# A decoder block on one core: one plain down slab split by two engines, and leftover differences and pair pieces put at other places

## The chip, the cores and the metric

The kernel runs on one core of a Trainium2 chip. A core has a matrix engine (TensorE, PE in the profile, with its weight loads as PEld), a vector engine (VectorE, DVE), a scalar engine (ScalarE, ACT), a general engine (GpSimd, POOL) and a sequencer that issues transfers (SyncE, SP). Each engine works through its own list of instructions in order and waits on semaphores for the others; DMA queues move data between memory and the on-chip buffers. The metric is the time of one execution on the device in microseconds; less is better.

## The reference

One layer of a decoder block over 512 tokens of width 1024, in float32. Two feed-forward halves (SwiGLU, hidden width 2816) enclose a convolution branch and a dilated attention branch; a gated embedding and a last norm follow. The two feed-forward halves are what the change touches:

```python
def swiglu(x, w_gate, w_up, w_down):
    return (jax.nn.silu(x @ w_gate) * (x @ w_up)) @ w_down
...
h = h + 0.5 * swiglu(rms_norm(h, g_ffn1[i]), w_ffn1_gate[i], w_ffn1_up[i], w_ffn1_down[i])
u = rms_norm(h, g_mix[i])
...
h = h + 0.5 * swiglu(rms_norm(h, g_ffn2[i]), w_ffn2_gate[i], w_ffn2_up[i], w_ffn2_down[i])
```

## The kernel before

**Numbers in two halves.** TensorE multiplies rounded numbers, so every operand is split into a rounded high half and the remainder, its low half, and each product is three matmuls: high by high, high by low, low by high. A weight slab of 128 x 1024 is therefore loaded raw (`wr`), and turned into `wh` and `wl`. There are two ways. In `split_one` ScalarE copies the slab into `wh` (rounding it) and VectorE subtracts: `wl = wr - wh` (lines 398 and 399 for products, 419 and 420 for other slabs). In `early_one`, for the slabs that `by_dma` names, ScalarE writes the rounded negative into `wl` (line 368), a DMA issued by POOL adds the raw slab to it on the way (line 370), and ScalarE makes `wh` (line 382). All of `wr`, `wh`, `wl` and some sums take one of 16 buffers of one pool (`NW`), which are handed on in the order in which they come free.

**Seven products for eight.** The gate, up and down products of the feed-forward halves are done in quarters with seven products, called B11, B21, T2, T1, T3, B22 and T4 (`PRODUCTS`). Each needs sums and differences of weight quarters (`sum_one`, VectorE, lines 336 to 349) and of the operands. T1 and T2 read the first differences of the operand, T3 and T4 the second ones. Products share banks of the accumulator: B11, T2, T3 and T4 use `pa`, B21 `pe`, T1 and B22 `pd`, so a product starts when VectorE or ScalarE has taken the one before out of its bank.

**The stages of one feed-forward half** (`ffn`). First come two plain pairs (`plain`, `EARLY` is 2): the first 256 hidden columns, gate and up, without the seven products, over eight chunks of 128 of the input, 6 matmuls each. At given chunks a hook runs: in the first half's second pair, `token` (the norm's statistics of each token, a chain of small VectorE operations that ends with eight diagonals, line 617) at chunk 0, `factor` (two matmuls, lines 622 and 623, that spread the factor over the partitions, and ScalarE's copy of it, `R`) at chunk 4, and `gate` (the products with the factor, silu and the products of gate and up, lines 831 to 834) at chunk 5. Meanwhile `forms` makes the first differences of the operand; its operations lie in the list `jobs`, from which `work` issues as many as fit the matmuls of a chunk by a count of what ScalarE and VectorE have already been given.

Then `PLAN` is followed: units of gate and up (`gu` 2 to 10), rounds of down (`dn` 1 to 5) and, around the last unit, the plain down of the pair that was made without the seven products (`dp` 0 0 and `dp` 0 1, one slab each, `down_plain`):

```python
PLAN = (("gu", 2), ("gu", 3), ("dn", 1), ... ("gu", 8), ("gu", 9),
        ("dn", 4), ("dp", 0, 0), ("gu", 10), ("dp", 0, 1), ("dn", 5))
```

`form_pair` prepares what a unit made for the down products: it lists its pieces in `later`: for B11, for B21 and B22, and for T1 and T2 and for T3 and T4 a ScalarE copy (line 688) and a VectorE split end (line 691) each, and four differences (line 676). The units issue them by `QUOTA` after each product; `down_plain` issues some with its second slab, and `down` forces those that a product still lacks.

**Loads and order.** `slab(key)` hands out the next slab and prepares those behind it in the order of `slab_order`: up to seven ahead are loaded by SP's queue, remainders go out by `LEAD` (5 slabs ahead for T4 and for `dp`, 3 for B11 and B21), and other slabs are split 2 ahead. The program's order is the order on each engine.

Of the kernel before, what the change touches and what calls it, by code (L numbers as in the profile page):

```python
# [22 lines left out]
KD = D // P  # L23
# [41 lines left out]
PRODUCTS = ("B11", "B21", "T2", "T1", "T3", "B22", "T4")  # L65
# [15 lines left out]
POOL_SUMS = False  # L81

POOLED = ("win", "v", "ao", "co")
RAISED = ("dp", "v0")
BY_DMA = ("B11", "B21", "T4")

N_GLU = (0, 0) + (6,) * 14
# [62 lines left out]
def block_kernel(ctx: ExitStack, tc: tile.TileContext, a, out):  # L150
# [44 lines left out]
    order = slab_order()  # L195
# [54 lines left out]
        return max(c.stop for _, c, _ in srcs)  # L250

    def by_dma(key):
        return (product(key) in BY_DMA or key[0] in POOLED + RAISED or key[:2] == ("gq", "2"))

    def product(key):
        return key[2] if key[0] in ("1", "2", "m") else None

    def W(n, dt=F32):
        return wts.tile([P, SLAB], dt, name=name(n), tag="w", bufs=NW)
# [10 lines left out]
    def row_of(srcs):  # L270
        at, out = 0, []
        for src in srcs:
            out.append((None, slice(at, at + src.shape[-1]), src))
            at += src.shape[-1]
        return out
# [85 lines left out]
    def spend(a_=0.0, v=0.0):  # L361
        spent[0] += a_
        spent[1] += v

    def remainder(l, h, srcs):

        spend(0.25 + l.shape[-1] * 0.00075)
        A.activation(l.bitcast(F32R), h, AF.Copy, scale=-1.0)  # L368
        for to, src in places(l, srcs):
            G.dma_start(to, src, accum_op=OP.add)  # L370

    def early_one():
        i = state["early"]
        state["early"] = i + 1
        if by_dma(order[i]):
            r = raws.pop(i)
            l = W("wl", F32R)[:, :r.shape[-1]]
            if product(order[i]) or order[i][0] in RAISED:
                h = W("wh", F32R)[:, :r.shape[-1]]
                remainder(l, r, row_of([r]))  # L380
                spend(0.25 + r.shape[-1] * 0.00075)
                A.activation(h, r, AF.Copy)  # L382
            else:
                h = r
                remainder(l, h.bitcast(F32), sources(order[i]))
            halves[i] = h, l
# [188 lines left out]
    class Norm:  # L575
# [5 lines left out]
        def add(self, t):  # L581
            sq = T("sq")
            A.activation(sq, t, AF.Square)
            self.flush()
            self.last = sq
# [61 lines left out]
    jobs, later = [], []  # L647
# [5 lines left out]
    def next_job(queue=None):  # L653
        f, a_, v = (queue or jobs or later).pop(0)
        if queue is not later:
            spend(a_, v)
        f()
# [9 lines left out]
    def form_pair(x1, x2, parts_, tile_=None, first_of=None, by=V):  # L667


        second, t = [], {"tile": tile_} if first_of is None else first_of  # L670

        def sub(o, half, p_, q_):
            def f():
                if o not in t:
                    t[o] = T("t")
                by.tensor_sub(t[o][:, half], p_(), q_())
            job(f, queue=later)

        def put(names, src):
            w, at = 256 * len(names), []  # L680

            def first_():
                if w == 256:
                    z = T("b", F32R)
                    at.extend((z[:, :256], z[:, 256:]))
                else:
                    at.extend((T("bh", F32R), T("bl", F32R)))
                A.activation(at[0], src(), AF.Copy)

            def end():  # L690
                V.tensor_sub(at[1], src(), at[0].bitcast(F32))
                for i, q in enumerate(names):
                    parts_[q] = tuple(z[:, i * 256:(i + 1) * 256] for z in at)
            job(first_, queue=later)
            second.append(lambda: job(end, queue=later))

        def next_():
            second.pop(0)()

        def t1():  # L700
            sub(0, lo, lambda: x1[:, hi], lambda: x1[:, lo])

        def t2():
            sub(0, hi, lambda: x2[:, hi], lambda: t[0][:, lo])

        def t34():
            sub(1, lo, lambda: x2[:, hi], lambda: x1[:, hi])
            sub(1, hi, lambda: x2[:, lo], lambda: t[0][:, hi])

        if x2 is None:  # L710
            put(("B11",), lambda: x1[:, lo])
            t1()
            next_()
            put(("T1",), lambda: t[0][:, lo])
            next_()
            return t
        if first_of is None:
            put(("B11",), lambda: x1[:, lo])
            put(("B21", "B22"), lambda: x2)
            t1()  # L720
            t2()
            next_()
            put(("T1", "T2"), lambda: t[0])
            next_()
            t34()
        else:
            t2()
            put(("B21", "B22"), lambda: x2)
            put(("T2",), lambda: t[0][:, hi])
            next_()  # L730
            t34()
            next_()
        if first_of is None:
            next_()
        put(("T3", "T4"), lambda: t[1])
        next_()
        job(t.clear, queue=later)
# [50 lines left out]
    def ffn(n, xs, u, norm, out_, soon_=None, last_=None):  # L788
# [95 lines left out]
        def token():  # L884
            y = norm.by_token()
            t = tiny("half", NB)
            V.tensor_scalar(t, y, 0.5, None, op0=OP.mult)
            half_r.append(t)
# [4 lines left out]
        def first():  # L893
            others.append(forms())

        def gate():
            rest = jobs[:]
            jobs.clear()
            gated(*done.pop(0))
            while jobs:  # L900
                next_job()
            jobs.extend(rest)

        done, others = [], []
        hooks = {(0, 1): {k: turns.pop(0) for k in range(KD)}, (1, 0): {0: token, 4: factor, 5: gate}} if n == "1" else {
            (0, 0): {2: soon_, 3: first}, (0, 1): {1: token, 6: factor}, (1, 0): {0: gate}}
        for j in range(EARLY):
            ps = []
# [66 lines left out]
        def down(r):  # L975

            at, k_ = ROUNDS[r]
            ps = banks()
            last = r == len(ROUNDS) - 1
            for q in PRODUCTS:  # L980
                wh, wl = slab((n, ("dn", r), q))
                for k in range(k_):
                    while q not in pairs.get(at + k, ()):
                        next_job(later)
                p = ps[BANKS[q]]
                rows_of(p, q, wh, wl, [pairs[at + k].pop(q) for k in range(k_)], last_[0] if last and q == "T4" else None)
                add(q, p, half_r[0])
                if last and q == "T4":
                    last_[1]()
                for f in ending:  # L990
                    f()
                ending[:] = [lambda q=q: finish(out_, q)] if last and q in FINAL else []
                work(k_ * 1.3)

        def down_plain(r, x_):
            at, k_ = (2 * z for z in ROUNDS[r])
            wh, wl = (z.rearrange("p (m k i) -> p k m i", m=4, k=k_) for z in slab(("dp", n, r, x_)))
            for two in ((0, 1), (2, 3)):
                while any(at + i not in hid for i in range(k_)):
                    next_job(later)  # L1000
                each = [(bank("pd"), b, slice(b * P, (b + 1) * P)) for b in two]
                for p, b, c in each:
                    for i in range(k_):
                        PE.matmul(p, hid[at + i][0][:, c], wh[:, i], start=i == 0, stop=False)
                        PE.matmul(p, hid[at + i][1][:, c], wh[:, i], start=False, stop=False)
                for p, b, c in each:
                    for i in range(k_):
                        PE.matmul(p, hid[at + i][0][:, c], wl[:, i], start=False, stop=i == k_ - 1)
                for _ in range(min(6 * x_, len(later))):
                    next_job(later)  # L1010
                for p, b, c in each:
                    t = h[b][:, x_ * S:(x_ + 1) * S]
                    V.scalar_tensor_tensor(t, p, half_r[0][:, b:b + 1], t, op0=OP.mult, op1=OP.add)
                spend(0, 1.5)
                work(2 * k_ * 0.68)
            if x_:
                hid.clear()
# [103 lines left out]
    turns = [lambda b=b, j=j: row_block(b, j) for j in (1, 0) for b in reversed(range(NB))]  # L1121
# [66 lines left out]
    for c in range(KD):  # L1188
        z = c, bank("pb"), bank("pa"), T("gg"), T("glu")
        if c == 0:  # L1190
            ws = [take(("win", m)) for m in (8, 0)]
            for k in range(KD):
# [4 lines left out]
                i = slice(k * P, (k + 1) * P)  # L1197
# [245 lines left out]
    for s in range(NSLOT):  # L1443
        q, k = [], []
# [4 lines left out]
        v0 = T("v0")  # L1449
# [13 lines left out]
        n = 1  # L1463
# [12 lines left out]
        v0 = None  # L1476
        q = k = None
# [79 lines left out]
    n = 0  # L1557
# [163 lines left out]
    for k in range(KD):  # L1721
        j, two = k % 2, (k // 2 * 2, k // 2 * 2 + 1)
# [84 lines left out]
```

## Time and profile before

| | us |
|---|---|
| Median of 3 runs | 1277.58 |
| Lowest and highest of them | 1277.21, 1277.71 |
| The profiled execution | 1279.57 |
| Its span, first to last instruction | 1277.8 |
| Granted TensorE clock, mean share | 0.996 |
| VectorE busy | 1051.6 |
| ScalarE busy | 743.3 |
| Software DMA queue (POOL's), share of 16 engines | 54.3% |

In the rows of a timeline the first number is the start in us from the start of the span, the second the time that the row's instructions take together, then come engine, line, operation, what is written from what, and a count; in brackets stands how long the engine was idle before and what ended that. In rows of waits the numbers after the colon are us in total, times and the longest. In a row of stretches the pairs are busy us and instructions of PE, PEld, DVE, ACT and POOL, then the granted TensorE clock, the DMA share and GB/s.

### The profile page before, as it was taken

How to read it: one execution, taken by the hardware profiler on the slowest of the kernel's cores; microseconds unless marked ns; L12 is line 12 of the kernel's file. 1: busy time of each engine (PE TensorE's matmuls, PEld its weight loads, DVE VectorE, ACT ScalarE, POOL GpSimd, SP SyncE). 2: the span in 40 equal slices, each digit the busy share in tenths (PEclk: the TensorE clock that was granted, in tenths of full speed). 3: DMA queues.
4: the chain of work that ended last, by engine and by line, in shares of the span. 5: the costliest groups of instructions: out<-in, count | busy, mean ns of one | idle time of the engine just before them, and what ended most of it. 6: DMA issues, size and time to landing. Idle time of an engine off the chain costs nothing.

```text
span 1277.8 us, 19737 instructions
## 1 busy us (share of the span) xinstructions
PE 1261.8 (99%) x7394; PEld 1118.8 (88%) x7394; DVE 1051.6 (82%) x1713; ACT 743.3 (58%) x1084; POOL 237.7 (19%) x310
## 2 busy tenths in 40 slices
PE   9999999999999999999999999999999999999997
PEld 7898999998888889889898888878898999998886
DVE  6898988897889988888888654797688988897975
ACT  6576666575643354747565545465576666665563
POOL 0011111111222232323332222124111111111000
PEclk9999999999999999999999999999999999999999
DMA  7378778688788899888888777759677778677531
GB/s 270 83 169 211 167 184 202 157 195 217 171 188 203 187 181 193 158 187 153 173 176 190 170 165 184 196 128 278 140 163 199 173 186 207 156 201 184 149 99 66
DMA packets 121702, 225.45 MB, mean 176 GB/s; under 512 B 19208, under 2 KB 63624, under 8 KB 121608
## 3 DMA queue, kind: packets, MB, share of 16 engines
q0 software_dynamic: 48160, 141.58, 54.3%
q1 hardware_dynamic: 73160, 82.37, 20.2%
q8 instruction: 58, 0.95, 0.3%
q14 instruction: 36, 0.29, 0.1%
q10 hardware_dynamic: 288, 0.26, 0.1%
HBM read 168.56 MB, written 2.13 MB: 134 GB/s over the span
## 4 chain that ended last, share of the span: by engine, by line
PE 88%; DVE 5%; DMA 2%; issue 2%; ACT 2%; DVEq 0%; POOLq 0%; ACTq 0%
PE pa L748 5%; PE pa L745 5%; PE pa L746 5%; PE pq L470 4%; PE pq L471 4%; PE pq L472 4%; PE pg L471 3%; PE pg L470 3%; PE pg L472 3%; PE pa L755 3%; PE pa L756 3%; PE pa L760 3%; PE pd L746 2%; PE pd L748 2%; PE pd L745 2%
## 5 line engine op out<-in xcount | busy, mean ns | idle before, releaser
L370 POOL DMA_DIRECT2D wl<-wr x98 | 84.6, 863 | 606.1 <-ACT wl L368 433.2
L1154 DVE SCALAR_TENSOR_TENSOR acc<-glu,taps,acc 128x511 f32<-128x511 f32 (+14 forms) x240 | 161.3, 733 | 0.0
L399 DVE TENSOR_TENSOR wl<-s,wh 128x1024 fp32r<-128x1024 f32 x90 | 109.9, 1221 | 41.6 <-ACT wh L398 32.2
L368 ACT ACTIVATE wl<-wh 128x1024 fp32r<-128x1024 f32 x84 | 87.9, 1051 | 72.8 <-DMA wh<-in_w_in 41.3
L368 ACT ACTIVATE wl<-wr 128x1024 fp32r<-128x1024 f32 x98 | 102.9, 1050 | 17.6 <-DVE wl L399 6.8
L745 PE MATMUL pa<-bh,wh 128*128 128x256 f32 x432 | 106.8, 285 | 3.2 <-DVE p L956 3.2
L382 ACT ACTIVATE wh<-wr 128x1024 fp32r<-128x1024 f32 x98 | 102.6, 1047 | 10.4 <-PE pd L760 7.4
L746 PE MATMUL pa<-bl,wh 128*128 128x256 f32 x432 | 106.7, 284 | 0.0
L398 ACT ACTIVATE wh<-s 128x1024 fp32r<-128x1024 f32 x90 | 94.0, 1049 | 21.2 <-PE pd L756 9.5
L370 POOL DMA_DIRECT2D wl<-in_w_in x56 | 48.7, 870 | 225.4 <-ACT wl L368 219.9
L470 PE MATMUL pq<-xsh,wh 128*128 128x512 f32 x224 | 88.7, 396 | 0.0
L471 PE MATMUL pq<-xsl,wh 128*128 128x512 f32 x224 | 87.3, 390 | 0.0
L472 PE MATMUL pq<-xsh,wl 128*128 128x512 f32 x224 | 87.3, 390 | 0.0
L745 PEld LDWEIGHTS pa<-bh,wh 128*128 128x128 f32 x432 | 83.3, 193 | 3.6 <-DVE p L956 3.6
L746 PEld LDWEIGHTS pa<-bl,wh 128*128 128x128 f32 x432 | 83.5, 193 | 0.0
L470 PE MATMUL pg<-xsh,wh 128*128 128x512 f32 x192 | 76.9, 401 | 0.3 <-DVE tg L831 0.2
L471 PE MATMUL pg<-xsl,wh 128*128 128x512 f32 x192 | 75.3, 392 | 0.7 <-DVE xsl L499 0.6
L472 PE MATMUL pg<-xsh,wl 128*128 128x512 f32 x192 | 75.0, 391 | 0.0
L943 ACT ACTIVATE p<-pa 128x512 f32<-128x512 f32 x36 | 21.5, 596 | 74.4 <-PE pa L748 74.0
L748 PE MATMUL pa<-bh,wl 128*128 128x256 f32 x432 | 61.4, 286 | 0.0
L771 DVE SCALAR_TENSOR_TENSOR gx<-pa,half,gx 128x512 f32<-128x512 f32 x80 | 56.3, 747 | 1.6 <-PE pa L760 1.3
L748 PEld LDWEIGHTS pa<-bh,wl 128*128 128x128 f32 x432 | 56.5, 195 | 0.0
(363 smaller groups left out, 3829.7 us busy)
## 6 DMA issues: line engine op xcount, KB each, us to landing
wl<-wr POOLq DMA_DIRECT2D x98, 512.0 KB, 5.2
wh<-in_w_in POOLq DMA_DIRECT2D x56, 512.0 KB, 7.3
wl<-in_w_in POOLq DMA_DIRECT2D x56, 512.0 KB, 6.5
wr<-in_w_ffn_down SPq DMA_DIRECT2D x44, 512.0 KB, 5.3
wr<-in_w_ffn_up SPq DMA_DIRECT2D x80, 256.0 KB, 4.5
wr<-in_w_ffn_gate SPq DMA_DIRECT2D x78, 256.0 KB, 4.9
wh<-in_w_v POOLq DMA_DIRECT2D x16, 256.0 KB, 7.1
wl<-in_w_v POOLq DMA_DIRECT2D x16, 256.0 KB, 5.1
```

The source lines that it names most:

```text
L368: A.activation(l.bitcast(F32R), h, AF.Copy, scale=-1.0)
L370: G.dma_start(to, src, accum_op=OP.add)
L382: A.activation(h, r, AF.Copy)
L398: A.activation(h, r, AF.Copy)
L399: V.tensor_sub(l, r, h.bitcast(F32))
L470: PE.matmul(ps, wh, xh, start=start, stop=False, skip_group_check=part)
L471: PE.matmul(ps, wh, xl, start=False, stop=False, skip_group_check=part)
L472: PE.matmul(ps, wl, xh, start=False, stop=stop, skip_group_check=part)
L745: PE.matmul(o, h[:, c], th, start=q in ("B11", "B21", "T1") and i == 0, stop=False, skip_group_check=True)
L746: PE.matmul(o, h[:, c], tl, start=False, stop=False, skip_group_check=True)
L748: PE.matmul(o, l[:, c], th, start=False, stop=i >= len(at) - 2, skip_group_check=True)
L1154: bg.append(lambda acc=acc, g=g, w=w, s=s: V.scalar_tensor_tensor(acc[:, s:], g[:, :S - s], w, acc[:, s:], op0=OP.mult, op1=OP.add))
```

## The change

Three things are changed.

The first slab of the plain down (`dp` 0 0, in both halves) leaves the names that are split with a DMA; `split_one` does it with ScalarE and VectorE, two slabs ahead. The second slab (`dp` 0 1) stays with the DMA.

In the second plain pair of the first half, the hook of chunk 0 first issues what is left of the first differences up to the last ScalarE copy, then `token`; `factor` and `gate` stand one chunk later.

In `form_pair` the split end of T1 and T2 stands ahead of the two second differences. With the second slab of the plain down, 2 pieces instead of 6 are issued after its second half, and up to 3 each after B11 and B21 of the last round of down.

```diff
-RAISED = ("dp", "v0")
+RAISED = ("v0",)
...
     def by_dma(key):
-        return (product(key) in BY_DMA or key[0] in POOLED + RAISED or key[:2] == ("gq", "2"))
+        return (product(key) in BY_DMA or key[0] in POOLED + RAISED or key[:2] == ("gq", "2")
+                or key[0] == "dp" and key[3])
...
-            if product(order[i]) or order[i][0] in RAISED:
+            if product(order[i]) or order[i][0] in RAISED + ("dp",):
...
             put(("T1", "T2"), lambda: t[0])
             next_()
+            next_()
             t34()
         else:
...
             t34()
-            next_()
-        if first_of is None:
             next_()
         put(("T3", "T4"), lambda: t[1])
...
+        def soon_first():
+            while any(a_ for _, a_, _ in jobs):
+                next_job()
+            token()
...
-        hooks = {(0, 1): {k: turns.pop(0) for k in range(KD)}, (1, 0): {0: token, 4: factor, 5: gate}} if n == "1" else {
+        hooks = {(0, 1): {k: turns.pop(0) for k in range(KD)}, (1, 0): {0: soon_first, 5: factor, 6: gate}} if n == "1" else {
...
                 add(q, p, half_r[0])
+                if last and q in PRODUCTS[:2]:
+                    for _ in range(min(3, len(later))):
+                        next_job(later)
...
-                for _ in range(min(6 * x_, len(later))):
+                for _ in range(min((6 if two[0] == 0 else 2) * x_, len(later))):
                     next_job(later)
```

## The prediction

> **What bounds the kernel now.** I read the page first, then the waits of TensorE over the whole span, then the timelines of the stretches in which those waits lie.
>
> ```profile
> span 1277.8 us, 19737 instructions
> PE 1261.8 (99%) x7394; PEld 1118.8 (88%) x7394; DVE 1051.6 (82%) x1713; ACT 743.3 (58%) x1084; POOL 237.7 (19%) x310
> ...
> PE pa L745 <- DVE p L956: 3.2, 2, 1.8
> ...
> PE pd L748 <- DVE wl L399: 1.0, 1, 1.0
> PE pa L755 <- DVE gx L771: 0.8, 1, 0.8
> ...
> PE R L623 <- DVE diag L617: 0.2, 1, 0.2
> ```
>
> TensorE is busy 99% of the span, and the kernel leaves its matmuls as they are. So the change can only win or lose at the few places where TensorE stands still (16 us in all, ramp and tail included), and an instruction that goes elsewhere is worth nothing. The rows name four such places near the edits: the second plain pair of the first FFN (L623), the last unit of each FFN (L956 twice, L399 once) and the last round of the first FFN (L771). I take the edits by these places.
>
> **The first differences and the token norm, first FFN.**
>
> ```profile
> 35.88 0.16 DVE L645 SCALAR_TENSOR_TENSOR m<-rows 128x4 f32<-128x4 f32 x1 [0.79 <-ACT sq L641]
> ...
> 39.34 0.88 DVE L617 TENSOR_SCALAR diag<-ident,yl 128x128 fp32r<-128x128 f32 x4
> ...
> 40.20 0.70 DVE L846 TENSOR_TENSOR bl<-t,bh 128x512 fp32r<-128x512 f32 x1
> ...
> 41.60 0.68 DVE L846 TENSOR_TENSOR bl<-t,bh 128x512 fp32r<-128x512 f32 x1
> ...
> 45.68 0.69 DVE L831 TENSOR_TENSOR tg<-pg,R 128x512 f32<-128x512 f32 x1
> ```
> ```profile
> 39.13 0.39 PE L472 MATMUL pu<-xsh,wl 128*128 128x512 f32 x1
> 39.58 0.47 PE L622 MATMUL R<-diag,one_r 128*128 128x512 f32 x1
> 40.28 0.50 PE L623 MATMUL R<-diag,one_r 128*128 128x512 f32 x1 [0.23 <-DVE diag L617]
> 40.62 0.39 PE L470 MATMUL pg<-xsh,wh 128*128 128x512 f32 x1
> ...
> 45.85 0.39 PE L472 MATMUL pu<-xsh,wl 128*128 128x512 f32 x1
> ...
> 46.42 0.50 PE L470 MATMUL pg<-xsh,wh 128*128 128x512 f32 x1 [0.18 <-DVE tg L831]
> ```
>
> From 40.62 to 45.85 are 23 matmuls, 0.227 us each. Three steps after 39.13 is 39.81, but the plain matmuls go on at 40.62: **0.81 us** are lost because factor's two matmuls (L622, L623) stand at chunk 4 and the diagonals are ready only at 40.2. At the next pair TensorE starts at 46.42 instead of 46.08, since its bank comes free with the first L831; the loss lies between the 0.18 of the row and 0.34, and I take **0.24**.
>
> The change puts one split end and two differences (40.20 to 41.60, 1.40 us) and one ScalarE copy (a later row) ahead of the token norm. VectorE stood idle 0.79 us before L645, so the norm starts 0.6 later at most and its last diagonal ends near 40.8. Factor now stands one chunk later, six matmuls or 1.36 us: at 40.72 for L622 and 40.95 for L623. Both find their diagonal; the margin is 0.1 to 0.2 us. Gate, too, moves one chunk back, to about 42.1, but what it waits for comes earlier:
>
> ```profile
> 41.72 0.63 ACT L843 ACTIVATE bh<-t 128x512 fp32r<-128x512 f32 x1 [5.87 <-DVE t L856]
> ```
>
> ScalarE sat 5.87 us behind this copy, with the split of the next slab and the copy of R queued after it. Issued before the norm it runs near 36.5, and VectorE's list after the norm is one split end, one slab subtraction and two split ends (0.6 + 1.14 + 1.2 from 40.8), so that L831 runs near 43.7 instead of 45.68. TensorE wants its bank at 45.3. No DMA is moved by this; SP's and POOL's queues keep their order. Both losses go: **-1.05 us**; the bounds are nothing and -1.15. Behind it no wait of TensorE is named until the last unit at 316 us, and its loads are released by TensorE itself, so the gain should travel.
>
> **The order of the pair's pieces and the quotas, last round of each FFN.**
>
> ```profile
> 328.09 0.68 DVE L691 TENSOR_TENSOR bl<-u,bh 128x512 fp32r<-128x512 f32 x1
> 328.69 0.42 DVE L676 TENSOR_TENSOR t<-u 128x256 f32<-128x256 f32 x1
> ...
> 330.75 1.40 DVE L1013 SCALAR_TENSOR_TENSOR gx<-pd,half,gx 128x512 f32<-128x512 f32 x2
> 332.07 1.22 DVE L399 TENSOR_TENSOR wl<-s,wh 128x1024 fp32r<-128x1024 f32 x1
> 333.21 1.40 DVE L771 SCALAR_TENSOR_TENSOR gx<-pa,half,gx 128x512 f32<-128x512 f32 x2
> ...
> 338.11 1.41 DVE L771 SCALAR_TENSOR_TENSOR gx<-pa,half,gx 128x512 f32<-128x512 f32 x2
> ```
> ```profile
> 332.22 1.07 PE L760 MATMUL pe<-wl,bh 128*128 128x512 f32 x4
> 334.10 0.47 PE L755 MATMUL pa<-wh,bh 128*128 128x512 f32 x1 [0.81 <-DVE gx L771]
> ...
> 337.09 0.39 PE L755 MATMUL pd<-wh,bh 128*128 128x512 f32 x1
> ```
>
> T2 could start at 332.22 + 4 x 0.227 = 333.13 and end 12 x 0.227 later, at 335.85; the next product starts at 337.09, so **1.24 us** are lost, to an add of B11 that VectorE begins at 333.21. Ahead of it VectorE does, between the two halves of the plain down, six pieces from 328.09 to 330.75 (2.66 us). With the new order and the quota of 2 it does two split ends there (0.60 each, as from 328.09 to 328.69), so the second half's add begins near 329.3, the slab subtraction near 330.6 and B11's add near 331.75. T2 then finds its bank. The other pieces (two differences of 0.33, one split end of 0.60) follow the adds of B11 and B21, still ahead of T3, the first to need them. VectorE has no slack here, so part comes back: counting on, T2's add ends near 339.3 as before, while T3 now wants the bank at 338.6 and its second half at 339.05: 0.4 us of new wait. Net **-0.85 us**, bounds 0 and -1.24. In the second FFN no L771 wait is shown, because TensorE already comes late there: 0. In the other units the same pieces only swap places within one quota: 0, hidden by VectorE's idle time.
>
> **The plain down's first slab.** Removed per FFN: one ScalarE copy, one POOL issue and its 512 KB DMA. Added: one VectorE subtraction, and the remaining copy moves two slabs later.
>
> ```profile
> 286.11 1.07 ACT L368 ACTIVATE wl<-wr 128x1024 fp32r<-128x1024 f32 x1 [0.75 <-PE pd L756]
> ```
> ```profile
> L420 DVE TENSOR_TENSOR wl<-wr,wh x9: 1215/1226/2023, 16.5 to 1215.6; 128x1024 fp32r<-128x1024 f32 x9
> ```
> ```profile
> 300.16 1.41 DVE L1013 SCALAR_TENSOR_TENSOR gx<-pd,half,gx 128x512 f32<-128x512 f32 x2 [1.31 <-PE pd L1008]
> ...
> 1160.92 1.41 DVE L1013 SCALAR_TENSOR_TENSOR gx<-pd,half,gx 128x512 f32<-128x512 f32 x2 [1.14 <-PE pd L1008]
> ```
>
> The subtraction takes 1.22 us, 1.14 in a row of others, right behind T3's add in the fourth round. Queued behind it are the sums for the last unit and the adds of B22, T4 and the first half; all are late by up to 1.1 us, and the idle 1.31 and 1.14 us before the second half's add swallow that. The matmuls that read the low half come some 5 us after it. So 0, with bounds of -0.3 and +1.1 in each FFN, were that cover gone. ScalarE's 1.05 us and POOL's issue free nobody: the next remainders there go out earlier, but no TensorE wait hangs on them.
>
> **What stays: the last unit.**
>
> ```profile
> 307.10 0.85 POOL L370 DMA_DIRECT2D wl<-wr  x1 [11.64 <-ACT wl L368]
> ```
> ```profile
> 314.96 1.23 DVE L399 TENSOR_TENSOR wl<-s,wh 128x1024 fp32r<-128x1024 f32 x1 [3.88 <-DMA wl<-wr]
> ...
> 1177.32 1.23 DVE L399 TENSOR_TENSOR wl<-s,wh 128x1024 fp32r<-128x1024 f32 x1 [5.48 <-DMA wl<-wr]
> ```
> ```profile
> 310.26 1.05 ACT L398 ACTIVATE wh<-s 128x1024 fp32r<-128x1024 f32 x1
> ...
> 313.10 0.59 ACT L943 ACTIVATE p<-pd 128x512 f32<-128x512 f32 x1
> ```
> ```profile
> 310.00:320.00 10.00, 8.60 (x72) 8.40 (x71) 6.12 (x10) 6.22 (x8) 1.70 (x2) 1.00 1.02 263
> ```
> ```profile
> 1181.00:1184.60 3.60, 3.00 (x18) 3.00 (x19) 3.56 (x6) 0.77 (x1) 0.86 (x1) 0.73 0.64 123
> 1184.60:1188.00 3.40, 3.40 (x17) 3.06 (x17) 3.40 (x5) 3.36 (x5) 0.86 (x1) 0.78 0.39 119
> ```
>
> The dear waits are here. B22's low half is written into a weight buffer that T4's remainder DMA still reads; VectorE stands 3.88 and 5.48 us for its landing, and TensorE then waits for the add behind it (1.4 and 1.8, and 1.0 before that in the second FFN). That DMA goes out at 307.10 beside the round's loads, long after the removed one (its copy at 286.11) has landed, and all of these are released by TensorE. I see nothing in the change that moves them relative to each other: 0. After the second of these waits the granted clock (the column ahead of the DMA share) is 0.73 over 3.6 us and 0.78 over 3.4 us, which costs 0.97 + 0.75 = 1.7 us more.
>
> **The sum** against the profiled execution (1279.57 us, of it span 1277.8): -1.05 - 0.85 = -1.9 us. It ran 2.0 us above the median of the runs, so I take the difference alone to the median: 1277.6 - 1.9 = **1275.7 us**, 0.15% less. A measurement of this kernel can tell about 0.2%, 2.6 us, from no change.
>
> **Rivals.**
>
> *Only one gain holds* (0.12). L623 has a margin of 0.1 to 0.2 us, and VectorE is full in the last round. Either gain alone gives 1276.5 to 1276.7.
>
> *The clock drop goes* (0.13). The second FFN's stands still come 1.9 us earlier, and if TensorE's clock then isn't lowered, 1.7 us go as well: 1274.0. For it: in the first FFN a wait of 1.4 us lowered nothing (granted clock 1.00 from 310 to 320). Against: the waits themselves stay. The Trainium skill (TensorE: Matmul & The Clock Gate, part 1) says that the clock is halved after an idle window of some 3.4 us, and that the windows run freely; by that no single wait here is long enough, yet the rows show the drop, worth 3.4 us at half rate, so its phase, not only the wait's length, seems to decide.
>
> *The landing in the last unit comes sooner* (0.12), with less DMA traffic ahead. If the second FFN's came like the first's (1.6 us sooner: 5.48 against 3.88 of idle), the 1.0 us wait and the clock's 1.7 go: 1273.0; without any such wait, a further 1.4 + 1.8 less: 1269.8. Against: the removed DMA ended long before.
>
> *Slower: B22's copy takes that buffer* (0.08). The removed tiles change the order in which the 16 weight buffers come round. If the one that T4's DMA reads falls to B22's high half (L398, now at 310.26) instead of the low one, ScalarE stands till 314.9, and behind it are a remainder's two copies and the L943 of 313.10, which has to empty pd before B22. L943 then ends near 318.5, B22 runs 2.9 us and T4 starts near 321.4, not 319.2: +2 us in each FFN, and the clock's 1.7 in the first: +5.7 - 1.9, 1281.4. It decides from the point where that buffer is freed one place earlier in the order. Against: I count the buffers to come round in the same order, two of them exchanged.
>
> *The edits change nothing that TensorE waits for* (0.05): 1277.6.
>
> **Chances.** The forecast holds 0.50, with a range of its own of 1274.9 to 1276.5; about 0.05 of it lies beyond 0.2%. Faster by over 0.2%: 0.05 + 0.13 + 0.12 = 0.30. Slower: 0.08, and 0.02 for the subtraction uncovered in both FFNs without the gains. Within: 0.60. The range leaves out the slow rival and the far end of the sooner landing: 1271.8 to 1278.2.
>
> **What would show it.** Right: in the changed profile no wait of L623 on L617, no 0.81 at L755 of T2 in the last round, L831 near 43.7, and L399's waits for DMA wl<-wr unchanged. Wrong: a wait of TensorE on the new subtraction, L398 waiting for a wl DMA in the last unit, or a PEclk of 1.0 after the second last unit.

## The result and the profile after

The changed kernel takes **1286.28 us** (median of 6 runs, 1283.34 to 1288.91) against 1277.64 us of the kernel before on the same chip (6 runs, 1277.21 to 1279.27): a ratio of 1.0066, with an interval from 1.0051 to 1.0081. It was forecast 0.15% faster; it is 0.66% slower. Line numbers from 253 to 725 have grown by one (L399 is now L400, L688 now L689), those from 734 to 893 are as before (L755, L760 and L771 among them), and the later ones have grown by five to eight.

First the page and the waits of TensorE of the changed kernel:

```profile
span 1281.6 us, 19727 instructions
PE 1261.4 (98%) x7394; PEld 1117.6 (87%) x7394; DVE 1053.8 (82%) x1715; ACT 742.6 (58%) x1082; POOL 236.8 (18%) x308
...
PE pe L760 <- DMA wl<-wr: 3.8, 3, 1.4
PE pa L755 <- ACT wh L399: 3.6, 2, 1.8
PE pa L745 <- DVE p L961: 1.9, 2, 1.4
```

TensorE's work is the same. The waits named for the start (L623, L831) and for T2's bank (L771) are gone, as forecast. Two new ones stand first: three waits for a remainder DMA at B21 (`pe`), and two at T3, one in each FFN.

Both traces hold 7394 matmuls. Taken in the order of their starts, the n-th of the one can be set beside the n-th of the other; the difference of the two starts shows where time is lost. The last column is the same for the last kernel of the experiments below.

| start in before, us | what has passed | after minus before, us | last kernel minus before, us |
|---|---|---|---|
| 47.00 | token norm of the first FFN | -1.14 | -1.12 |
| 102.10 | up to B21 of round one | -0.74 | -0.81 |
| 104.14 | B21 of round one | +0.66 | -0.81 |
| 280.01 | up to B21 of round four | +0.67 | -0.81 |
| 283.19 | B21 of round four | +2.39 | -0.81 |
| 330.18 | the last unit | +1.50 | +0.13 |
| 339.58 | T2 of the last round | +0.26 | -1.11 |
| 342.07 | T3 of the last round | +2.48 | -0.63 |
| 1140.09 | second FFN, up to round four's B21 | +3.06 | +0.37 |
| 1142.13 | B21 of round four | +4.61 | +0.37 |
| 1189.05 | the last unit | +1.55 | -3.10 |
| 1202.19 | T2 of the last round | +1.55 | -3.09 |
| 1210.00 | T3 of the last round | +3.78 | -2.61 |

So B21 costs 1.40 + 1.72 + 1.55 = 4.67 us in three rounds, and T3 2.22 + 2.23 = 4.45 us. Against this stand the start (1.14), T2 (1.24) and the last units. Two smaller losses lie between the rows. Of the 1.14 us, 0.40 are gone before round one; the kernel with the hook alone loses 0.33 there too, and neither trace names a cause. Behind T3 of the first FFN another 0.70 are lost at 350.89, where a plain product waits 0.43 us for a DMA (L473 on `wl<-in_w_in`): ScalarE prepares the first two remainders of that stage at 341.84 and 345.18, in the kernel before at 338.68 and 340.12. No other kernel here has this wait.

The table compares the two profiled executions, which are 3.8 us apart. The medians are 8.6 us apart: the profiled execution of the kernel before lies 1.9 us above its median, that of the changed kernel 2.9 us below.

**Why B21 waits.** ScalarE's timeline before round four, first of the kernel before, then of the changed one:

```profile
270.87 0.63 ACT L688 ACTIVATE bh<-t 128x512 fp32r<-128x512 f32 x1 [0.91 <-DVE t L676]
271.40 1.05 ACT L368 ACTIVATE wl<-wr 128x1024 fp32r<-128x1024 f32 x1
```
```profile
273.87 0.63 ACT L689 ACTIVATE bh<-t 128x512 fp32r<-128x512 f32 x1 [3.25 <-DVE t L677]
274.41 1.04 ACT L369 ACTIVATE wl<-wr 128x1024 fp32r<-128x1024 f32 x1
```

VectorE's rows, first of the kernel before, then of the changed one, and TensorE's of the changed one:

```profile
270.08 0.42 DVE L676 TENSOR_TENSOR t<-u 128x256 f32<-128x256 f32 x1
270.41 0.42 DVE L676 TENSOR_TENSOR t<-u,t 128x256 f32<-128x256 f32 x1
270.75 1.22 DVE L340 TENSOR_TENSOR s<-s,wr 128x1024 f32<-128x1024 f32 x1
```
```profile
271.35 0.42 DVE L677 TENSOR_TENSOR t<-u 128x256 f32<-128x256 f32 x1
271.69 1.22 DVE L341 TENSOR_TENSOR s<-s,wr 128x1024 f32<-128x1024 f32 x1
272.82 0.68 DVE L961 TENSOR_TENSOR p<-p,pa 128x512 f32<-128x512 f32 x1
273.42 0.42 DVE L677 TENSOR_TENSOR t<-u,t 128x256 f32<-128x256 f32 x1
```
```profile
282.71 1.20 PE L760 MATMUL pe<-wl,bh 128*128 128x512 f32 x4 [1.41 <-DMA wl<-wr]
```

The copy of the second differences (L689) needs both of them. Before, VectorE made them one behind the other. In the new order the second one stands on VectorE behind a sum of weights (L341) and an add, and is done at 273.8. ScalarE stands 3.25 us for it, and the copy behind, which prepares B21's remainder for its DMA (L369), goes out 3.0 us later than before (274.41 against 271.40; only 0.67 of that is TensorE's own lateness). The DMA then lands after B21's matmuls want it.

**Why T3 waits.** The last round of the first FFN: ScalarE of the kernel before, then ScalarE, VectorE and TensorE of the changed one.

```profile
329.48 0.63 ACT L688 ACTIVATE bh<-t 128x512 fp32r<-128x512 f32 x1 [2.30 <-DVE t L676]
330.02 1.99 ACT L398 ACTIVATE wh<-s 128x1024 fp32r<-128x1024 f32 x2
```
```profile
328.58 1.04 ACT L399 ACTIVATE wh<-s 128x1024 fp32r<-128x1024 f32 x1
335.33 0.63 ACT L689 ACTIVATE bh<-t 128x512 fp32r<-128x512 f32 x1 [5.71 <-DVE t L677]
335.87 1.04 ACT L399 ACTIVATE wh<-s 128x1024 fp32r<-128x1024 f32 x1
```
```profile
334.88 0.42 DVE L677 TENSOR_TENSOR t<-u,t 128x256 f32<-128x256 f32 x1
336.95 1.23 DVE L400 TENSOR_TENSOR wl<-s,wh 128x1024 fp32r<-128x1024 f32 x1 [1.65 <-ACT wh L399]
338.09 1.40 DVE L771 SCALAR_TENSOR_TENSOR gx<-pe,half,gx 128x512 f32<-128x512 f32 x2
...
341.14 1.40 DVE L771 SCALAR_TENSOR_TENSOR gx<-pa,half,gx 128x512 f32<-128x512 f32 x2
```
```profile
342.04 0.47 PE L755 MATMUL pa<-wh,bh 128*128 128x512 f32 x1 [1.81 <-ACT wh L399]
```

The same copy again: it is the third piece issued after B11, and T1's split (the L399 of 335.87) stands behind it. ScalarE does nothing for 5.71 us, then VectorE nothing for 1.65 us, because its half of that split needs ScalarE's. Every add behind is late, T2's among them (341.14), and T3 needs the bank that this add empties. The row names ACT L399, but T3's high half was there from 339.8 on (the split of 338.72); 342.04 is 0.9 us into the L771 of 341.14, whose first half takes 0.7. In the kernel before, T2 started 0.89 us into the L771 that held its bank (334.10 against 333.21), and there the row names the add. So the engine named in a wait for several semaphores has to be checked against its own rows.

**The last unit** of the second FFN, stretches of the changed kernel (the prediction has the same two of before):

```profile
1181.00:1184.60 3.60, 2.22 (x19) 2.01 (x17) 3.60 (x7) 1.72 (x3) 0.00 (x0) 1.00 0.66 131
1184.60:1188.00 3.40, 3.36 (x26) 3.32 (x27) 3.37 (x5) 1.13 (x2) 0.86 (x1) 1.00 0.61 116
```

The granted clock is 1.00 here, where before had 0.73 and 0.78. This gives back the 1.7 us that the prediction priced, but not as a rule: the mean clock of this execution, 0.998, is the highest of the six runs of the changed kernel (the others 0.995 to 0.997), and its time, 1283.34 us, the lowest. One such drop, 1.7 us of 1284, lowers the mean clock by 0.0013, so the others would have had one or two of them, worth 1.7 to 3.4 us (an estimate; they have no trace). What else spreads these runs, 1285.41 us at 0.995 and 1288.91 at 0.996, is not shown.

### The profile page after: what moved, and what is told of

Same layout as the page of the kernel before. It is cut to its first block, busy times and chain, and to the rows that moved or that the text cites. A ratio compares the mean times of both kernels' runs of the same rounds, so it can differ in the third digit from the quotient of the medians.

```text
span 1281.6 us, 19727 instructions
## 1 busy us (share of the span) xinstructions
PE 1261.4 (98%) x7394; PEld 1117.6 (87%) x7394; DVE 1053.8 (82%) x1715; ACT 742.6 (58%) x1082; POOL 236.8 (18%) x308
## 4 chain that ended last, share of the span: by engine, by line
PE 78%; issue 8%; DVE 6%; DMA 4%; ACT 2%; POOL 1%; DVEq 0%; POOLq 0%; ACTq 0%
PE pa L748 5%; PE pa L746 5%; PE pa L745 5%; PE pq L471 4%; PE pq L472 4%; PE pq L473 4%; PE pa L755 2%; PE pa L756 2%; PE pa L760 2%; PE pd L748 2%; PE pd L746 2%; PE pd L745 2%; PE pg L472 2%; PE pg L473 2%; PE pg L471 2%
## 5 line engine op out<-in xcount | busy, mean ns | idle before, releaser
L400 DVE TENSOR_TENSOR wl<-s,wh 128x1024 fp32r<-128x1024 f32 x90 | 109.8, 1220 | 42.5 <-ACT wh L399 35.6
L369 ACT ACTIVATE wl<-wh 128x1024 fp32r<-128x1024 f32 x84 | 87.9, 1052 | 72.1 <-DMA wh<-in_w_in 38.7
L369 ACT ACTIVATE wl<-wr 128x1024 fp32r<-128x1024 f32 x96 | 100.7, 1049 | 16.4 <-DVE wl L400 5.7
L399 ACT ACTIVATE wh<-s 128x1024 fp32r<-128x1024 f32 x90 | 94.1, 1049 | 22.8 <-PE pd L756 8.5
L473 PE MATMUL pq<-xsh,wl 128*128 128x512 f32 x224 | 87.3, 390 | 0.0
L473 PE MATMUL pg<-xsh,wl 128*128 128x512 f32 x192 | 75.0, 391 | 0.0
L755 PE MATMUL pa<-wh,bh 128*128 128x512 f32 x136 | 53.6, 394 | 3.6 <-ACT wh L399 3.6
L771 DVE SCALAR_TENSOR_TENSOR gx<-pa,half,gx 128x512 f32<-128x512 f32 x80 | 56.2, 744 | 1.0 <-PE pa L760 0.8
```

Source lines behind the costliest of these rows:

```text
L400: V.tensor_sub(l, r, h.bitcast(F32))
L473: PE.matmul(ps, wl, xh, start=False, stop=stop, skip_group_check=part)
```

## The experiments

The theory after the result: the loss is ScalarE's copy of the second differences, issued too soon behind VectorE's second difference, with other work queued behind it, at two places: in the units (order) and in the last round (quota). The rivals: the slab split, or weight buffers and DMAs that come round otherwise.

**One part of the change at a time** (before on the same chip: 1278.55 us, 31 runs). The hook alone:

```diff
-(1, 0): {0: token, 4: factor, 5: gate}
+(1, 0): {0: soon_first, 5: factor, 6: gate}
```

> Only the hook of the second plain pair is changed. Theory (the loss comes from the copy of the T3/T4 differences, which now stands on ScalarE ahead of the difference that it waits for, with slab copies behind it): this part has no share in the loss, TensorE's waits at 40 and 46 us go, and nothing is added: -1.0 us, 1276.5. Rival (each part loses by moving the landings of DMAs): slower than before by 2 us or more, with new waits of TensorE on DMA wl<-wr.

1277.77 us, ratio 0.9999 (0.9987 to 1.0012). The waits at L623 and L831 are gone and the matmul that started at 47.00 starts 1.06 earlier; by round one 0.73 are left. In the timed runs that can't be told from nothing. No wait for B21.

The slab split alone:

```diff
-RAISED = ("dp", "v0")
+RAISED = ("v0",)
...
+                or key[0] == "dp" and key[3])
```

> Only the plain down's first slab is split by ScalarE and VectorE. Theory: VectorE's two idle times before the plain down's second add hide the subtraction, 0 +- 0.5 us, no new wait of TensorE. Rival (the added subtraction makes VectorE late in round four and the last unit): +2 us or more, with TensorE waits on VectorE in round four or the plain down.

1278.8 us, ratio 1.0007 (0.9995 to 1.0019): nothing that can be told, and no TensorE wait on the new subtraction. This rival falls as the main cause.

The new order of the pieces alone, in all units:

```diff
             put(("T1", "T2"), lambda: t[0])
             next_()
+            next_()
             t34()
```

> Only the order of the pair's pieces is changed. Theory: the copy of the T3/T4 differences waits on ScalarE in the ninth unit of both halves, B21's remainder of round four goes out some 3 us later, TensorE waits 1.3 to 1.4 us for it in each half: +2.5 to +4 us in all, and spread between runs of more than 1.5 us. No new wait in round one (the pieces aren't shifted by one without the hook) and the 0.8 us wait at T2 in the last round stays. Rival (the new order alone is harmless, the quotas or the slab lose): within 1 us of before.

1283.15 us, ratio 1.0032 (1.002 to 1.0044), 4.6 us above before and so somewhat more than expected. Its waits of TensorE:

```profile
PE pa L754 <- DVE gx L770: 2.8, 2, 1.4
PE pe L759 <- DMA wl<-wr: 2.8, 2, 1.5
```

Round four's two waits for B21 belong to the order; round one's isn't here. T2's wait in the last round, expected to stay at 0.8 us in the first FFN, is 1.4 in both. The quotas alone:

```diff
+                if last and q in PRODUCTS[:2]:
+                    for _ in range(min(3, len(later))):
+                        next_job(later)
...
-                for _ in range(min(6 * x_, len(later))):
+                for _ in range(min((6 if two[0] == 0 else 2) * x_, len(later))):
```

> Only the quotas around the last round are changed, the order stays. Theory: the copy of the T3/T4 differences comes behind B11's add, ScalarE stands some 5 us, T1's split comes late and TensorE waits about 1.8 us at T3 in each half, against 0.8 at T2 in the first before: +2 to +3.5 us. Rival (the quotas do what was predicted): -0.8 us, no wait over 0.5 at T3.

1280.08 us, ratio 1.0017 (1.0007 to 1.0028), with `PE pa L755 <- ACT wh L398` 1.2 us twice: the wait at T3 belongs to the quotas. It is shorter than the 1.8 us expected, and the time, 1.5 us above before, a little below the range. The four parts add up to 0.55%, the whole has 0.66% (0.51 to 0.81).

**Is it the place in the list?** A pair has 13 pieces, and the units issue 4, 2, 1, 3, 3 and 3 after B11, B21, T2, T1, T3 and B22 (`QUOTA`), 16 in all. Unit 8 has four pieces more, of the plain pair (two copies and two split ends of `hid`), so one piece is left over, `t.clear`, which does nothing on the chip but takes the first place in unit 9. Counted out with this shift, the old order has both second differences after T1 and their copy after T3. The new one has the first difference after T1, and the second one and the copy both after T3. Without the shift it, too, has both differences after T1 and the copy after T3. So the new order was run with the clearing done in the last split end, 12 pieces (before on this chip: 1279.0 us, 35 runs):

```diff
-        put(("T3", "T4"), lambda: t[1])
+        put(("T3", "T4"), lambda: t[1], t.clear)
         next_()
-        job(t.clear, queue=later)
```

> This kernel has the new order of the pair's pieces in every unit, as the kernel of the order alone, but the clearing of T3's and T4's operands is done together with their split end, so that a pair has 13 pieces as before minus one and none is left over for the next unit. Theory (a piece left over shifts every later piece by one place, so ScalarE's copy of the differences is issued before VectorE can do the second difference, and B21's remainder copy stands behind it): the waits of TensorE for the remainder DMA of B21 in round four (1.5 us each half, 2.8 in all with the order alone) are gone; the last round keeps its wait for T1's add (about 1.4 us each half), since the copy is followed there by its split end; the time is 1279 to 1281, +1 to +2.5 us on before. Rival (the order itself, by its DMA landing or its weight buffers, is what costs): as the order alone, 1282 to 1284, with the waits for B21's remainder still there.

1278.86 us, ratio 1.0000 (0.9991 to 1.0009). The waits for B21 are gone, and ScalarE's copy there starts at 271.01 after 0.33 us of idle, not 3.25. The order by itself costs nothing that can be told (0.09% at most); its place against the quota does. The time came out slightly below what was expected: of the two waits in the last round (T2's for B11's add, which the expectation calls T1's) one stayed (1.4), the other is not shown.

**Is it ScalarE's queue in the last round?** The change's quotas, and the new order for the last pair only, once with three pieces after B11 (the copy ahead of T1's split), once with two (behind it):

```diff
-            form_pair(*ts, pairs[j], tile_)
+            form_pair(*ts, pairs[j], tile_, ends=j == KF // 2 - 1)
...
-                    for _ in range(min(3, len(later))):
+                    for _ in range(min({"B11": 2, "B21": 3}[q], len(later))):
```

The second part of this cut is the difference between the two kernels, early and late.

> The new order for the last pair only, with the change's quotas (two pieces in the plain down, three after B11, three after B21), and neither the hook nor the slab split. ScalarE's copy of T3's and T4's differences is the third piece after B11 and so ahead of T1's split in ScalarE's queue. Theory (that copy holds T1's split until VectorE's second difference is done): TensorE waits 1.2 to 1.8 us at T3 in each FFN, as in the changed kernel, and no wait for B21's remainder in rounds one and four; 1279 to 1281, +1.5 to +3 us on before. Rival (the quota of two delays nothing; the waits of the changed kernel's last round come from the hook's or the slab's shift): the wait at T3 is below 0.5 and the time within 1 us of before.

> As the kernel with the copy early, but two pieces after B11 and three after B21, so that ScalarE's copy of the differences is issued behind T1's split. Theory: T1's split no longer waits for VectorE; the wait at T3 is at most 0.5 us, the wait at T2 of before (0.8) is gone, and the time is 1276.5 to 1278.5, about 0.8 us below before. Rival (the second difference and the adds themselves fill VectorE in that round): the wait at T3 stays at 1.2 or more and the time at 1279 to 1281.

Early 1282.33 us, ratio 1.0028 (1.0019 to 1.0038), late 1278.24 us, 0.999 (0.9979 to 1.0001). ScalarE's timeline, early and then late:

```profile
333.86 0.63 ACT L688 ACTIVATE bh<-t 128x512 fp32r<-128x512 f32 x1 [5.71 <-DVE t L676]
334.40 1.04 ACT L398 ACTIVATE wh<-s 128x1024 fp32r<-128x1024 f32 x1
```
```profile
329.99 1.06 ACT L398 ACTIVATE wh<-s 128x1024 fp32r<-128x1024 f32 x1 [0.42 <-PE pd L1010]
...
335.44 0.63 ACT L688 ACTIVATE bh<-t 128x512 fp32r<-128x512 f32 x1 [1.67 <-DVE t L676]
```

One piece moved past one split is worth 0.38% of the timed runs with the same work: T1's split runs 4.4 us sooner, and TensorE's waits lose their row for T3 (2.3 us in two in the early one). VectorE's adds and differences are the same in both, so a full VectorE isn't the cause. By the starts of the matmuls, early loses 2.2 and 0.4 us more than late at the two T3s; the rest of the 4.4 us between the two traces lies in the last units, where early has one drop of the clock more (1.7 us). Early came out above what was expected (1279 to 1281).

With the hook added to the late one (no slab split):

> The hook of the change, the new order in the last pair only, and the quotas with ScalarE's copy behind T1's split; no slab split. Theory: both gains that the prediction counted come without the price, 1275 to 1277.5, about 1.9 us below before: no waits at L622 and L623, none of T2, none over 0.5 at T3, none for B21's remainder in rounds one and four. Rival (the hook alone shifts the pieces of unit three so that B21 waits in round one of the first FFN): a wait of 1.1 us there and a time of 1277 to 1279.

1276.82 us, ratio 0.9978 (0.9967 to 0.999), against 0.999 without the hook on the same chip: 1.5 us, where 1.1 was counted, though the intervals touch. No wait for B21 in round one: with the old order in that unit the hook does no harm.

**The changed kernel itself, with each of the two places put right** (before on this chip: 1278.24 us, 24 runs): the clearing merged, two pieces instead of three after B11, and both. Their edits are those above.

> The changed kernel, with the clearing of T3's and T4's operands done together with their split end (12 pieces for a pair, none left over in the second last unit but one). Theory: the waits of TensorE for B21's remainder in round four (1.4 and 1.3 us) are gone in both FFNs; the wait of round one of the first FFN (1.1), to which the hook's shift of the pieces leads, stays or goes; the waits at T3 (1.8 each) stay. 1280 to 1283.5, ratio to before 1.001 to 1.0045, some 3 us below the changed kernel. Rival (round four waits because of the DMA's landing or of the buffers' order): its waits stay and the ratio is 1.005 to 1.008.

> The changed kernel with two pieces instead of three after B11 of the last round, so that ScalarE's copy of the differences is issued behind T1's split. Theory: the waits at T3 (1.8 each) fall to 0.5 or less in both FFNs, and those for B21's remainder (1.1, 1.4 and 1.3) stay; 1280 to 1283.5, ratio 1.001 to 1.0045. Rival (T3 waits because VectorE's adds and differences fill that round): its waits stay and the ratio is 1.005 to 1.008.

> The changed kernel with both of these edits. If the two placements of ScalarE's copy are the whole of the loss, only the wait of round one in the first FFN can be left (1.1): 1276 to 1278.5 at the level of 1278.5 of before, ratio 0.998 to 1.0. If something else in the change costs too, the ratio stays above 1.001 and the rest has its own row in the waits of TensorE.

| changed kernel | us | ratio to before | waits for B21 | waits at T3 |
|---|---|---|---|---|
| as it is | 1286.28 | 1.0066 (1.0051 to 1.0081) | 3.8 in three | 3.6 in two |
| clearing merged | 1281.26 | 1.0024 (1.0013 to 1.0035) | none | 2.3 in two |
| two after B11 | 1282.19 | 1.0041 (1.0023 to 1.0059) | 3.8 in three | none |
| both | 1276.95 | 0.999 (0.9981 to 0.9999) | none | none |

These are the waits that TensorE's rows name. By the starts of the matmuls one T3 still comes some 0.5 us late in each of the two kernels at the end of the table; no row names a cause.

Each edit takes its own wait and leaves the other; together they take 0.76%, 9.7 us, and the interval of the kernel with both takes in the forecast (0.9985). Round one's wait goes with the merging too: there, by the order of the instructions, the hook makes the pair's pieces begin one product later, so that a piece is left over, and the new order makes that dear. Neither does so alone (the hook alone and the order alone had no such wait); the two without the rest of the change were not run. What is left in TensorE's waits with both edits is what before had:

```profile
PE pa L745 <- DVE p L961: 2.9, 2, 1.8
...
PE pd L748 <- DVE wl L400: 0.8, 1, 0.8
```

Last, the hook, the slab split, and the order and the late quotas for the last pair only:

> The hook, the slab split, and the new order and the late quotas in the last pair only: the kernel with the hook and the late copy (0.9978 of before) plus the slab split. Theory (the split is hidden): 0.997 to 0.9985, the same waits as without the split, no wait of TensorE on the new subtraction or on the adds behind it. Rival (VectorE's 1.2 us there are no longer covered once TensorE comes earlier): 0.9985 to 1.0, with waits of up to 1.1 us at B22 or T4 of the last unit.

1276.97 us, ratio 0.9989 (0.998 to 0.9998): a little above the range expected for a hidden split, and not to be told from the kernel without the split (0.9978) or the one with both edits (0.999). It waits nowhere for the subtraction (L421). Its time lies in the range of the rival (0.9985 to 1.0), but TensorE's longest wait for VectorE at B22 of the last units is 0.3 us, not 1.1. What the split itself is worth stays open: alone it measured between 0.05% faster and 0.19% slower.

## Why the prediction was wrong

- **The hook: right, with one consequence missed.** VectorE's and TensorE's rows of the changed kernel:

```profile
39.97 0.87 DVE L618 TENSOR_SCALAR diag<-ident,yl 128x128 fp32r<-128x128 f32 x4
40.85 0.39 PE L623 MATMUL R<-diag,one_r 128*128 128x512 f32 x1
41.08 0.40 PE L624 MATMUL R<-diag,one_r 128*128 128x512 f32 x1
43.76 0.68 DVE L831 TENSOR_TENSOR tg<-pg,R 128x512 f32<-128x512 f32 x1
```

  The diagonals are found without a wait, L831 runs at 43.76 (43.7 was forecast), and 1.14 us are won (1.05). That the gain "should travel" failed: 0.40 us are lost again before round one, and the hook also moves pieces to other places, for which round one pays 1.40.
- **"In the other units the same pieces only swap places within one quota: 0, hidden by VectorE's idle time": this step failed.** It is worth +4.67 us. The pieces do not stay within one quota where a piece is left over, and the engine whose queue decides is ScalarE, whose copy holds a remainder's copy, POOL's issue and a DMA behind it. VectorE's idle time hides nothing of that.
- **"The other pieces (two differences of 0.33, one split end of 0.60) follow the adds of B11 and B21": this step failed too.** Between the differences and the split end lies ScalarE's copy. Counted as the third piece it stands ahead of T1's split. T2 gave back 1.24 us, to the digit (+1.50 to +0.26 in the table), but T3 took 2.22, not 0.4. Where the copy stands behind the split, T3 takes 0.48 in the last kernel (-1.11 to -0.63), 0.51 in the changed kernel with two pieces after B11 and nothing in the three others, while T2 gives back 1.24 in all five. So the sizes were about right for another quota than the one in the diff.
- **"In the second FFN ... 0"**: T3 took 2.23 us there as well, and at most 0.50 in the five kernels with the late copy. T2's gain was rightly nothing; the price at T3 does not need that gain.
- **The slab split at 0** is borne out within 0.2% by the kernel with the split alone.
- **The last unit at 0** held for the mechanism, not for the size. The waits there shrink where TensorE comes later: the changed kernel comes 2.39 us late and loses 0.89 less than before. The rival of the clock drop came true in the profiled execution; the lower mean clocks of the other five suggest that it didn't there.
- **The slower rival** was another one: no ScalarE split waits for B22's buffer in the last unit. A rival for ScalarE's queue was lacking, though the prediction itself shows its pattern: 5.87 us before the L843 of 41.72, "with the split of the next slab and the copy of R queued after it".

The Trainium skill (TensorE: Matmul & The Clock Gate, Part 1, "Architectural detail") says that ScalarE's queue is strictly first in, first out. The rows agree: the split of 335.87 starts only when the copy ahead of it has its operand, while with the copy behind it the same split ran at 329.99.

## What to carry to other kernels

When pieces of a list are put in another order, write down for each its engine and what its engine has queued behind it, and count out the list against the quotas with whatever is left over from the stage before; a piece that does nothing on the chip still takes a place. A copy on one engine that reads another engine's result belongs at least one quota behind it, and behind any split that the next product needs. "The same work in another order" is nothing only when each engine's queue has been followed.

## What the runs showed of the clock

Two kernels have the same waits in the last unit of the first FFN. Timeline of TensorE and stretches, first the merged order, then the late copy:

```profile
317.58 1.22 PE L747 MATMUL pd<-xsh,wl 128*128 128x256 f32 x8 [0.54 <-DVE wl L399]
...
320.59 0.39 PE L744 MATMUL pa<-bh,wh 128*128 128x256 f32 x1 [1.79 <-DVE p L955]
```
```profile
318.00:322.00 4.00, 2.21 (x18) 2.01 (x17) 4.00 (x7) 2.52 (x3) 0.85 (x1) 1.00 0.45 94
322.00:326.00 4.00, 4.00 (x26) 3.59 (x25) 3.96 (x7) 2.37 (x3) 0.49 (x1) 1.00 0.71 135
```
```profile
317.65 1.21 PE L750 MATMUL pd<-xsh,wl 128*128 128x256 f32 x8 [0.52 <-DVE wl L399]
...
320.65 0.48 PE L747 MATMUL pa<-bh,wh 128*128 128x256 f32 x1 [1.79 <-DVE p L958]
```
```profile
318.00:322.00 4.00, 2.21 (x14) 2.00 (x13) 4.00 (x6) 2.52 (x3) 0.85 (x1) 0.85 0.60 123
322.00:326.00 4.00, 4.00 (x23) 3.85 (x23) 3.96 (x7) 2.30 (x3) 0.42 (x1) 0.73 0.57 109
```

Waits of 0.54 and 1.79 us leave the clock at 1.00; waits of 0.52 and 1.79, at the same distance, bring it to 0.85 and 0.73, which costs 0.15 x 4 + 0.27 x 4 = 1.7 us. So the lengths of the waits alone don't decide.

The packed traces, which note each change of the granted clock, show what does. Apart from the start and the end of the span, the clock is halved for 3.41 us at a time (once for two such stretches in a row), and the times between its changes are whole multiples of 3.413 us in all 14 traces. The marks of that grid lie elsewhere in each trace, at 6.76 us of the span in the late copy and at 5.81 in the merged order. Cut at these marks, the same two waits fall into one stretch in the one kernel and into two in the other:

| trace | stretch, us | TensorE busy in it | granted clock of the next stretch |
|---|---|---|---|
| late copy | 317.37 to 320.78 | 39% | 0.50 |
| merged order | 316.42 to 319.83 | 54% | 1.00 |
| merged order | 319.83 to 323.25 | 78% | 1.00 |
| kernel before, second FFN | 1179.27 to 1182.68 | 47% | 0.50 |
| changed kernel, second FFN | 1181.16 to 1184.57 | 60% | 1.00 |

In the 14 traces eleven stretches at full clock have TensorE busy for 48% or less, and each is followed by one at half clock; none with 52% or more is. (In the early copy a stretch that itself ran at half clock, 82% busy, is followed by another.) What lies between 48 and 52% no trace shows.

The Trainium skill (TensorE: Matmul & The Clock Gate, Part 1) says that the clock is judged over windows of some 3.4 us that run freely, and that an idle window halves it. The traces agree with the windows and their free run. They differ on the condition: the stretches before the drops are 36 to 48% busy, not idle.
